# A two-layer diffusion backbone on one core: FFN up-projection as seven block products, FFN in two phases

## Chip, core, metric

One core of one Trainium2 chip. The metric is the device time of one execution in microseconds (us); lower is better. Engines: TensorE (PE; its weight loads are PEld), VectorE (DVE), ScalarE (ACT), GpSimd (POOL), and SyncE (SP), which issues the DMAs.

## What is computed

Two layers act on 512 latent tokens and 256 context tokens of width 1024. Each layer is a mixing sublayer (three groups of heads, one output projection) and a gated FFN with a hidden width of 2816. The last layer's FFN runs on the 512 latent tokens only; layer 0's runs on all 768.

```python
def swiglu(h, w13, w2):
    gate, up = jnp.split(h @ w13, 2, axis=-1)
    return (jax.nn.silu(gate) * up) @ w2
...
for l in range(DEPTH):
    ...
    lat = lat + gt1 * rms_norm(mixed_l, norm_mix_post[l])
    h_l = modulate(rms_norm(lat, norm_ffn_pre[l]), sh2, sc2)
    lat = lat + gt2 * rms_norm(swiglu(h_l, ffn_w13[l], ffn_w2[l]), norm_ffn_post[l])
```

## The kernel before

**Precision.** Every large product is made of three matmuls. An operand is split into a high part (a cast to the matmul's format, done by ACT) and a low part (operand minus high part, done by DVE or POOL); `gemm3` (L383 to L388) then accumulates high·high, high·low and low·high in PSUM.

**Weights.** Weights stream in units of at most 1 MB, in the order of a list (`specs`). `load` (L307 to L329) fetches a unit into `raw` (one buffer), casts `whi` (L327, ACT, up to 2048 columns in one instruction) and subtracts `wlo` (L328, DVE); both have two buffers. `get` (L331) loads one unit ahead.

**Normalized input.** `pre_norm` (L246 to L267) normalizes a tile of 128 tokens, turns it by 8 transposes on PE (L256), applies scale and shift while it leaves PSUM (`hh`, half on ACT, half on DVE) and writes high and low parts into `hT` (ACT L266, POOL L267), which holds all tokens. The output projection is software-pipelined: while PE works on a tile, the tile before is normalized (`out_front`, `out_back`).

**FFN.** The hidden width is 22 blocks of 128. `ffn_up` computes gate and up of a block for all tokens: in layer 0, 48 matmuls of 512 columns (latent tokens) and 48 of 256 (context); in layer 1, 48 of 512. The first two blocks (`ffn_first`) are cut into 256-token pieces, so that they start with the tokens that are already normalized. `ffn_gate` makes silu(gate) (ACT L1130) times up (DVE L1131); `ffn_split` makes the hidden block's high part (ACT L1135) and low part (POOL L1136), which stay in SBUF. After each group of blocks (groups of 2, 4, 4, 4, 4, 4) `ffn_down` multiplies the group by its 512-column halves of `ffn_w2`; a group's result is added to `facc` in SBUF (ACT L1181 for the first, DVE L1183 for the others). In the last group each tile's post-norm, and in layer 0 the pre-norm of layer 1, follow the tile's two halves (`ffn_back`).

**Order.** A tile scheduler places the instructions on the engines' queues from program order; each engine then runs its own queue in order. Side work, the matmuls of the modulation vectors (`pa`, L196 to L210, with 512 KB DMAs `araw`), is put in between at hand-placed points (`ada_some`).

Of the kernel before, what the change touches and what calls it, by code (L numbers as in the profile page):

```python
# [20 lines left out]
D = 1024  # L21
# [62 lines left out]
def tile_backbone(ctx: ExitStack, tc: tile.TileContext, a: dict, out: bass.AP, dbg=None):  # L84
# [5 lines left out]
    wp = ctx.enter_context(tc.tile_pool(name="wp", bufs=2))  # L90
# [37 lines left out]
    hT = [pt(pp, "hThi", [128, 8, T], F32R), pt(pp, "hTlo", [128, 8, T], F32R)]  # L128
    hTf = [h.bitcast(F32) for h in hT]
# [7 lines left out]
    qds = [pt(dp, f"qd{l}", [T, 512]) for l in range(NL)]  # L137

# [107 lines left out]
    def pre_norm(np_, l, k, tb, x):  # L246
# [4 lines left out]
        for j in range(2):  # L251
            ps = px()
            h = pt(np_, "hh", [128, 4, 128])
# [53 lines left out]
    def load(i, hp=None, tag=None):  # L307
        name, shape, srcs, prem, hook = specs[i]
# [3 lines left out]
        rs = f"p ({dims}) -> p {dims}"  # L312
        hp = hp or wp
        lo = pt(hp, "wlo", [128, 2048], F32R)[:, :n].rearrange(rs, **kw)
        hi = pt(hp, "whi", [128, 2048], F32R)[:, :n].rearrange(rs, **kw)
        raw = pt(wp, "raw", [128, 2048], bufs=1)[:, :n].rearrange(rs, **kw)
# [4 lines left out]
        if prem is not None:  # L321
            for kb in range(shape[1]):
                w = cols[prem][:, 66 + kb:67 + kb]
                S.activation(hi[:, kb], raw[:, kb], AF.Copy, scale=w)
                V.scalar_tensor_tensor(lo[:, kb], raw[:, kb], w, hi.bitcast(F32)[:, kb], ALU.mult, ALU.subtract)
        else:
            S.copy(hi, raw)  # L327
            V.tensor_tensor(lo, raw, hi.bitcast(F32), ALU.subtract)  # L328
        state["units"][i] = (hi, lo)  # L329
# [17 lines left out]
    for l in range(NL):  # L347
# [895 lines left out]
```

## Time and profile before

| | |
|---|---|
| median of 3 runs | 1917.22 us (1916.05 to 1921.72) |
| span of the profiled execution | 1910.3 us |
| time of the profiled execution | not given apart from its span; 6.9 us lie between span and median |
| PE busy | 1834.0 us, 96% of the span, 11579 matmuls |
| DVE, ACT, POOL busy | 906.6 us (47%), 670.5 us (35%), 436.5 us (23%) |

The span runs from the first to the last instruction of the execution. Busy time of matmuls is modelled and they overlap in the pipeline, so the time that one matmul costs in a stream is read from the chain of waits (a piece's length by its count), not from its mean duration.

### The profile page before, as it was taken

What the parts mean: (1) busy time and instruction counts of PE and PEld (TensorE: products, weight loads), DVE (VectorE), ACT (ScalarE), POOL (GpSimd) and SP (SyncE); (2) the same over time, 40 slices, a digit from 0 to 9 for tenths busy, and PEclk for the clock granted to TensorE, in tenths of its full rate; (3) what the DMA queues carried; (4) which work ended last, traced back from release to release, by engine and by line L of the source; (5) the groups of instructions that cost most, each with busy time, mean ns of one, the idle gap of its engine ahead of it and who ended that gap; (6) DMA issues with size and microseconds to landing.
All of it is one profiled execution on the core that took longest, in us unless ns stands there. A gap on an engine that the chain in (4) does not pass through costs nothing.

```text
span 1910.3 us, 28279 instructions
## 1 busy us (share of the span) xinstructions
PE 1834.0 (96%) x11579; PEld 1562.8 (82%) x11579; DVE 906.6 (47%) x1594; ACT 670.5 (35%) x1157; POOL 436.5 (23%) x413
## 2 busy tenths in 40 slices
PE   5999999999999999999999989999997999999998
PEld 3789988878998888888888767898896987888886
DVE  4576698747432222322223265739876432332334
ACT  3545453225533212121121265545333542222222
POOL 1103454205321111111010131046322231112112
PEclk9899999999999999999999998999997999999999
DMA  8335344546352222222222363343423343333232
GB/s 281 114 111 161 114 144 139 176 148 218 132 165 87 68 77 78 66 63 70 67 89 62 93 214 102 97 138 112 133 86 108 110 159 110 88 102 97 89 90 87
DMA packets 242941, 221.71 MB, mean 116 GB/s; under 512 B 12024, under 2 KB 218844, under 8 KB 242684
## 3 DMA queue, kind: packets, MB, share of 16 engines
q1 hardware_dynamic: 241744, 218.60, 36.3%
q8 instruction: 91, 1.49, 0.3%
q10 hardware_dynamic: 1068, 1.31, 0.2%
q14 instruction: 38, 0.31, 0.1%
HBM read 197.99 MB, written 21.89 MB: 115 GB/s over the span
## 4 chain that ended last, share of the span: by engine, by line
PE 80%; DVE 9%; DMA 4%; ACT 3%; issue 2%; POOL 1%; SPq 0%; POOLq 0%; DVEq 0%; ACTq 0%
PE mm L388 46%; PE px L388 22%; PE pa L196 2%; PE px L906 2%; DVE wlo L328 1%; DMA araw<-ada_w_dram 1%; DVE W L672 1%; PE px L256 1%; PE px L635 1%; DMA vd<-stg 1%; ACT whi L327 1%; DVE E L666 1%; DMA xa<-x_dram 1%; PE px L844 1%; PE px L840 1%
## 5 line engine op out<-in xcount | busy, mean ns | idle before, releaser
L388 PE MATMUL mm<-hThi,whi 128*128 128x512 f32 (+2 forms) x1384 | 483.9, 350 | 4.0 <-ACT hThi L443 3.5
L388 PE MATMUL mm<-hTlo,whi 128*128 128x512 f32 (+2 forms) x1384 | 481.9, 348 | 3.0 <-DVE hTlo L444 2.3
L388 PE MATMUL mm<-hThi,wlo 128*128 128x512 f32 (+2 forms) x1384 | 481.2, 348 | 0.3 <-DVE wlo L328 0.2
L327 ACT CAST whi<-raw 128x2048 fp32r<-128x2048 f32 (+2 forms) x96 | 177.4, 1848 | 430.6 <-PE mm L388 197.2
L388 PEld LDWEIGHTS mm<-hThi,whi 128*128 128x128 f32 (+1 forms) x1384 | 260.1, 188 | 52.5 <-issue 8.7
L328 DVE TENSOR_TENSOR wlo<-raw,whi 128x2048 fp32r<-128x2048 f32 (+2 forms) x96 | 216.8, 2258 | 171.2 <-ACT whi L327 170.9
L388 PEld LDWEIGHTS mm<-hTlo,whi 128*128 128x128 f32 (+1 forms) x1384 | 260.4, 188 | 42.7 <-DVE hTlo L444 2.6
L1136 POOL TENSOR_TENSOR hidlo<-hf,hidhi 128x768 fp32r<-128x768 f32 (+1 forms) x44 | 126.6, 2878 | 731.8 <-ACT hidhi L1135 731.8
L388 PEld LDWEIGHTS mm<-hThi,wlo 128*128 128x128 f32 (+1 forms) x1384 | 260.5, 188 | 37.6 <-DVE wlo L328 1.4
L1131 DVE TENSOR_TENSOR hf<-mm,hf 128x512 f32<-128x512 f32 (+1 forms) x63 | 37.7, 598 | 397.7 <-PE mm L388 387.5
L388 PE MATMUL mm<-whi,hThi 128*128 128x256 f32 x688 | 200.7, 292 | 5.6 <-ACT stg L747 3.2
L388 PE MATMUL mm<-whi,hTlo 128*128 128x256 f32 x688 | 198.4, 288 | 0.0
L388 PE MATMUL mm<-wlo,hThi 128*128 128x256 f32 x688 | 198.2, 288 | 0.0
L388 PE MATMUL px<-wlo,hidhi 128*128 128x512 f32 x440 | 174.6, 397 | 0.0
L388 PE MATMUL px<-whi,hidhi 128*128 128x512 f32 x440 | 174.5, 398 | 0.0
L388 PE MATMUL px<-whi,hidlo 128*128 128x512 f32 x440 | 174.0, 397 | 0.0
L388 PEld LDWEIGHTS mm<-whi,hThi 128*128 128x128 f32 x688 | 131.8, 192 | 15.8 <-ACT stg L747 5.1
L388 PEld LDWEIGHTS mm<-wlo,hThi 128*128 128x128 f32 x688 | 131.8, 192 | 2.9 <-issue 1.9
L388 PEld LDWEIGHTS mm<-whi,hTlo 128*128 128x128 f32 x688 | 131.7, 191 | 2.7 <-issue 1.9
L1183 DVE TENSOR_TENSOR facc<-facc,px 128x512 f32<-128x512 f32 x100 | 68.2, 685 | 129.1 <-PE px L388 129.1
L1130 ACT ACTIVATE hf<-mm 128x512 f32<-128x512 f32 (+1 forms) x63 | 32.9, 522 | 246.9 <-PE mm L388 246.9
L388 PEld LDWEIGHTS px<-whi,hidhi 128*128 128x128 f32 x440 | 83.2, 189 | 20.5 <-issue 0.8
(270 smaller groups left out, 2852.5 us busy)
## 6 DMA issues: line engine op xcount, KB each, us to landing
araw<-ada_w_dram SPq DMA_DIRECT2D x96, 512.0 KB
raw<-ffn_w_dram SPq DMA_DIRECT2D x92, 512.0 KB
raw<-w_in_dram SPq DMA_DIRECT2D x26, 1024.0 KB
raw<-ffn_w_dram SPq DMA_DIRECT2D x20, 1024.0 KB
Rt<-gd SPq DMA_DIRECT2D x40, 256.0 KB
raw<-w_out_dram SPq DMA_DIRECT2D x8, 1024.0 KB
xsd<-x SPq DMA_DIRECT2D x16, 512.0 KB
x<-xsd SPq DMA_DIRECT2D x14, 512.0 KB
```

The source lines that it names most:

```text
L196: PE.matmul(ps[32 * g:32 * g + 32, 0:256], sil[:, 4 * kq + g, :], raws[kq][:, g, :], start=kq == 0, stop=kq == 1)
L256: PE.transpose(ps[:, 128 * q:128 * q + 128], xn[:, 128 * kb:128 * kb + 128], ident)
L327: S.copy(hi, raw)
L328: V.tensor_tensor(lo, raw, hi.bitcast(F32), ALU.subtract)
L388: PE.matmul(ps, x(k), y(k), start=(k == 0 and p == 0), stop=(k == n - 1 and p == 2))
L635: PE.matmul(pst[:, 256 * g:256 * g + 256], bt[:, 128 * g:128 * g + 128], xw[:, 256 * g:256 * g + 256], start=True, stop=True)
L666: V.scalar_tensor_tensor(E[:, h], Rt[:, 0, h], gcol[:, tb, hh:hh + 1], E[:, h], ALU.subtract, ALU.min)
L906: PE.matmul(ps[h][:, cs], XX[rr, 1, cs], XX[rr, 0, cs], start=True, stop=True)
L1130: S.activation(hf[:, t0:t0 + n], pg[:, :n], AF.Silu)
L1131: V.tensor_tensor(hf[:, t0:t0 + n], pu[:, :n], hf[:, t0:t0 + n], ALU.mult)
L1136: G.tensor_tensor(hh[1], hf, hh[0].bitcast(F32), ALU.subtract)
L1183: V.tensor_tensor(ac, ac, ps, ALU.add)
```

## The change

**Seven products.** For each hidden block the weights are split into four: a11, a12 are the gate's columns for the lower and upper half of the 1024 inputs, a21, a22 those of up. The normalized input is split into b11, b12 (lower inputs, first and second half of the tokens) and b21, b22 (upper inputs). Sums s1 to s4 of the weights and t1 to t4 of the input are formed, and seven products replace eight; each is 4 input blocks by 3 matmuls of half the tokens (384 columns in layer 0, 256 in layer 1), so 84 matmuls per block. The results are put together from PSUM and SBUF by ACT and DVE, multiplied on POOL, and the hidden block is stored to DRAM (`hds`).

**Weights.** Weights are split in halves of 1024 columns, with four buffers in place of two. `load13` fetches a block's four quarters by two DMAs of 512 KB, forms s3 and a21+a22 on POOL, s2 and s4 on DVE, and splits 3584 columns in four pieces (2048 before).

**FFN start.** `hT` gives way to a rotating pool `H`; the normalized FFN input is held whole in F32 (`whole`), and after the last tile it is turned into 7 operands with high and low parts and 4 differences, each in two halves.

**Down phase.** When all 22 blocks are stored, `hid_pair` reads two blocks at a time back from DRAM, once for each 512-column half of the output, splits them (ACT; DVE and POOL), and `down` accumulates all blocks in PSUM, one bank per tile, with no additions in SBUF. The first half is copied to `y0`; post-norms follow the tiles of the second half's last group.

```diff
-    wp = ctx.enter_context(tc.tile_pool(name="wp", bufs=2))
+    wp = ctx.enter_context(tc.tile_pool(name="wp", bufs=4))
...
+    hds = [pt(dp, f"hd{l}", [NF, 128, T if l + 1 < NL else TL]) for l in range(NL)]
...
+    def load13(i, srcs):
+        F = state["F"]
+        raw = wtile(wp if i % 2 else F, "raw", [128, 4, 512])
+        for dsl, src in srcs:
+            DMA.dma_start(raw[:, dsl].rearrange("p s (k n) -> p (s k) n", n=128), src)
+        a21, a22, a11, a12 = (raw[:, q] for q in range(4))
+        sm = pt(F, "S", [128, 3, 512], bufs=1)
+        s2, s3, s4 = (sm[:, q] for q in range(3))
+        G.tensor_tensor(s3, a11, a21, ALU.subtract)
+        G.tensor_tensor(a21, a21, a22, ALU.add)
+        V.tensor_tensor(s2, a21, a11, ALU.subtract)
+        V.tensor_tensor(s4, a12, s2, ALU.subtract)
+        t0 = split(wp, raw[:, 2:4], [128, 2, 512], V)
+        t1 = split(wp, sm[:, 0:2], [128, 2, 512], V)
+        t2 = split(wp, raw[:, 0:2], [128, 2, 512], V)
+        t3 = split(wp, sm[:, 2:3], [128, 1, 512], V)
...
+            rsplit("b11", bhi[:, 0], blo[:, 0], b11, V)
+            rsplit("b21", bhi[:, 1], blo[:, 1], b21, V)
+            vsub(t1, b12, b11)
+            vsub(t2, b22, t1)
+            vsub(t3, b22, b12)
+            vsub(t4, b21, t2)
+            rsplit("b22", bhi[:, 2], blo[:, 2], b22, V)
+            tlo = pt(hp, "H", [128, 4, 4, hn], F32R)
+            for nm, q in (("t2", 1), ("t3", 2), ("t1", 0), ("t4", 3)):
+                rsplit(nm, thi[:, q], tlo[:, q], tm[:, q], V)
...
+                pa = mm()
+                prod(pa, un, "a11", "b11", True)
+                uu = ut("uu")
+                S.copy(uu, pa[:, :hn])
+                pb = px()
+                prod(pb, un, "s2", "t2", True)
+                V.tensor_tensor(uu, uu, pb[:, :hn], ALU.add)
+                pc = px()
+                prod(pc, un, "s3", "t3", True)
+                u3 = ut("u3")
+                V.tensor_tensor(u3, uu, pc[:, :hn], ALU.add)
+                pd = px()
+                prod(pd, un, "s1", "t1", True)
+                V.tensor_tensor(h2, u3, pd[:, :hn], ALU.add)
+                prod(pa, un, "a12", "b21", False)
+                g1 = ut("g1")
+                S.activation(g1, pa[:, :hn], AF.Silu)
+                prod(pc, un, "a22", "t4", False)
+                V.tensor_tensor(h1, uu, pc[:, :hn], ALU.add)
+                G.tensor_tensor(h1, h1, g1, ALU.mult)
+                prod(pd, un, "s4", "b22", False)
+                V.tensor_tensor(uu, uu, pd[:, :hn], ALU.add)
+                g2 = ut("g1")
+                S.activation(g2, uu, AF.Silu)
+                G.tensor_tensor(h2, h2, g2, ALU.mult)
+                DMA.dma_start(hds[l][f], hf)
...
+            def hid_pair(f):
+                hr = pt(Dp, "hr", [128, 2, tot], bufs=2)
+                DMA.dma_start(hr, hview[:, f:f + 2])
+                hh = [pt(Dp, t, [128, 2, tot], F32R, bufs=3) for t in ("hidhi", "hidlo")]
+                for q in range(2):
+                    S.copy(hh[0][:, q], hr[:, q])
+                    (G if q else V).tensor_tensor(hh[1][:, q], hr[:, q], hh[0][:, q].bitcast(F32), ALU.subtract)
+                return hh
...
+            for j in range(2):
+                pss = accs(j)
...
+                        for k0 in range(0, gn, 2):
+                            hh = hid_pair(f + k0)
+                            for pos in range(npos):
+                                down(pss[pos], hh, un, k0, pos, f + k0)
```

Where the FFN of layer 0 begins, TensorE's queue before: `px_5907` and `px_5919` take the last tile's transposes, `mm_6042` and `mm_6043` are gate and up of the first block on the context tokens, `px_6094` its gate on the first 256 latent tokens.

```order
L388 MATMUL mm_6042<-hTlo_84,whi_6035 128x256
L388 MATMUL mm_6042<-hThi_83,wlo_6034 128x256 [waits DVE_49]
L388 MATMUL mm_6042<-hThi_83,whi_6035 128x256
L388 MATMUL mm_6042<-hTlo_84,whi_6035 128x256 [waits Pool_49]
...
L210 MATMUL pa_5996<-cst_75,arow_6005 128x2 [waits Activation_49]
L388 MATMUL mm_6043<-hThi_83,wlo_6034 128x256
L256 MATMUL px_5907<-cst_75,xn_5905 128x128 [waits Activation_49]
L256 MATMUL px_5907<-cst_75,xn_5905 128x128 x3
L256 MATMUL px_5919<-cst_75,xn_5905 128x128 x4
L388 MATMUL px_6094<-hThi_83,whi_6035 128x256
L388 MATMUL px_6094<-hTlo_84,whi_6035 128x256 [waits Pool_49]
```

Now: `px_5948` and `px_5957` take the last tile's transposes, `mm_6158` is a11·b11 and then a12·b21 of the first block, `px_6173`, `px_6187` and `px_6202` are the products with t2, t3 and t1 (`H_6071` their high parts, `H_6092` their low parts).

```order
L203 MATMUL pa_6050<-araw_6046,sil_102 32x256 x3
L266 MATMUL px_5948<-cst_75,xn_5946 128x128 [waits Activation_49]
L266 MATMUL px_5957<-cst_75,xn_5946 128x128 x4
L1211 MATMUL mm_6158<-bhi_6068,whi_6117 128x384 [waits Activation_49]
L1211 MATMUL mm_6158<-blo_6069,whi_6117 128x384 [waits DVE_49]
L1211 MATMUL mm_6158<-bhi_6068,wlo_6118 128x384 [waits DVE_49]
...
L1211 MATMUL px_6173<-H_6071,whi_6121 128x384 [waits Activation_49]
L1211 MATMUL px_6187<-H_6071,whi_6121 128x384
L1211 MATMUL px_6202<-H_6071,whi_6125 128x384 [waits Activation_49]
L1211 MATMUL mm_6158<-bhi_6068,whi_6117 128x384 [waits Activation_49]
L1211 MATMUL mm_6286<-bhi_6068,whi_6141 128x384 [waits Activation_49]
L1211 MATMUL px_6173<-H_6092,whi_6121 128x384 [waits DVE_49]
```

Before, matmuls of the FFN stood ahead of the last transposes; now every product stands behind them, and the first that uses a low part of a t stands behind the two halves of the first gate product.

At the same place DVE's queue now: L274 writes the last tile's normalized input (`H_4983` is `whole`), L1194 forms t1 to t4 in `tm_6070`, L1190 subtracts low parts (`blo_6069` of b, `H_6092` of t), L329 and L369, L370 are the first block's weights.

```order
L274 TENSOR_SCALAR H_4983<-px_5948,modc0_134 128x128 [waits Activation_49]
L1194 TENSOR_TENSOR tm_6070<-H_4983 128x768 [waits DMAHW0_49,DVE_49,Pool_49]
L1190 TENSOR_TENSOR blo_6069<-H_4983,bhi_6068 128x768 [waits DMAHW5_49,DMAHW2_49,Activation_49]
...
L1190 TENSOR_TENSOR blo_6069<-H_4983,bhi_6068 128x768 [waits Activation_49]
L329 TENSOR_TENSOR wlo_6118<-raw_6109,whi_6117 128x1024 [waits DMAHW1_49,Activation_49]
L369 TENSOR_TENSOR S_6112<-raw_6109 128x512 [waits DMAHW0_49,Pool_49]
L329 TENSOR_TENSOR wlo_6122<-S_6112,whi_6121 128x1024 [waits Activation_49]
L329 TENSOR_TENSOR wlo_6126<-raw_6109,whi_6125 128x1024 [waits Activation_49]
L329 TENSOR_TENSOR wlo_6130<-S_6112,whi_6129 128x512 [waits Activation_49]
L1190 TENSOR_TENSOR H_6092<-tm_6070,H_6071 128x768 [waits DVE_49]
L1190 TENSOR_TENSOR H_6092<-tm_6070,H_6071 128x768 x6
```

None of the L1194 and L1190 rows stood there before; `px_6173`'s wait on DVE above is for the first row that writes `H_6092`.

Where the up phase of layer 0 ends, SP's queue now: `hf` is a finished hidden block on its way to DRAM (`hd0_100`), `raw` a unit of `ffn_w2`, `hr` a pair of blocks on its way back.

```order
L342 DMA raw_8821<-ffn_w2_dram 128x2x512 [waits DMAHW3_49,DMAHW6_49,DMAHW2_49,DVE_49]
L1246 DMA hd0_100<-hf_8717 128x768 [waits DMAHW7_49,Pool_49]
L342 DMA raw_8946<-ffn_w2_dram 128x4x512 [waits DMAHW6_49,DMAHW0_49,DVE_49]
L1246 DMA hd0_100<-hf_8831 128x768 [waits DMAHW1_49,Pool_49]
L1258 DMA hr_8956<-hd0_100 128x2x768 [waits PE_49]
L342 DMA raw_9000<-ffn_w2_dram 128x4x512 [waits DMAHW0_49,DVE_49]
```

Before, SP had no hidden block to move; now the first pair's load stands behind the last block's store.

## Rows read from the trace of the kernel before

**Rows 1.** The page, part 1: busy time of each engine.
```profile
PE 1834.0 (96%) x11579; PEld 1562.8 (82%) x11579; DVE 906.6 (47%) x1594; ACT 670.5 (35%) x1157; POOL 436.5 (23%) x413
```

**Rows 2.** Part 4: the chain that ended last, by engine and line.
```profile
PE 80%; DVE 9%; DMA 4%; ACT 3%; issue 2%; POOL 1%; SPq 0%; POOLq 0%; DVEq 0%; ACTq 0%
PE mm L388 46%; PE px L388 22%; PE pa L196 2%; PE px L906 2%; DVE wlo L328 1%; DMA araw<-ada_w_dram 1%; DVE W L672 1%; PE px L256 1%; PE px L635 1%; DMA vd<-stg 1%; ACT whi L327 1%; DVE E L666 1%; DMA xa<-x_dram 1%; PE px L844 1%; PE px L840 1%
```

**Rows 3.** Stretches: both FFNs, an idle spell, the passage between layers.
```profile
core 0: us, PE busy (x) PEld busy (x) DVE busy (x) ACT busy (x) POOL busy (x), PEclk, DMA share, GB/s
532.50:1080.00 547.50, 544.96 (x2991) 459.19 (x2991) 137.68 (x147) 115.02 (x132) 76.30 (x29) 1.00 0.26 78
1528.00:1893.60 365.60, 363.60 (x1657) 296.72 (x1656) 120.25 (x106) 99.11 (x104) 68.80 (x30) 1.00 0.34 102
539.80:547.00 7.20, 4.66 (x32) 3.22 (x32) 2.30 (x5) 2.17 (x4) 1.93 (x3) 0.76 1.05 321
1094.50:1158.20 63.70, 53.17 (x332) 40.81 (x332) 33.26 (x63) 40.35 (x75) 22.33 (x30) 0.87 0.66 222
```

**Rows 4.** The chain by time (start, length, what): unbroken FFN streams.
```profile
560.54 14.95 PE px L388 x126
...
632.82 17.04 PE mm L388 x96
...
1576.97 44.99 PE mm L388 x192
```

**Rows 5.** The same chain where the FFN of layer 0 begins.
```profile
532.71 2.60 PE mm L388 x21
...
536.42 6.87 DMA araw<-ada_w_dram
...
544.35 1.90 PE px L256 x8
...
546.25 2.10 PE px L388 x15
```

**Rows 6.** The same chain where the FFN of layer 1 begins.
```profile
1526.23 5.05 DMA raw<-ffn_w_dram
...
1535.67 2.88 PE pa L388 x22
...
1538.55 0.60 PE px L256 x4
```

**Rows 7.** Instructions by line and shape (count, busy us, mean ns).
```profile
L328 DVE TENSOR_TENSOR wlo<-raw,whi 128x1024 fp32r<-128x1024 f32 x4 | 5.2, 1311 | 6.7 <-ACT whi L327 6.5
...
L1183 DVE TENSOR_TENSOR facc<-facc,px 128x512 f32<-128x512 f32 x100 | 68.2, 685 | 129.1 <-PE px L388 129.1
...
L444 DVE TENSOR_TENSOR hTlo<-xT,hThi 128x768 fp32r<-128x768 f32 x4 | 3.8, 956 | 1.0 <-ACT hThi L443 0.8
...
L1131 DVE TENSOR_TENSOR hf<-mm,hf 128x256 f32<-128x256 f32 x22 | 9.3, 424 | 52.5 <-PE mm L388 42.3 <-issue 10.2
...
L327 ACT CAST whi<-raw 128x1024 fp32r<-128x1024 f32 x4 | 4.2, 1048 | 11.7 <-PE mm L388 9.0 <-DMA raw<-ffn_w_dram 2.7
...
L681 POOL TENSOR_TENSOR y<-xs,dsk 128x512 f32<-128x512 f32 x10 | 10.5, 1056 | 106.8 <-DMA Rt<-gd 96.5 <-DVE z L700 10.3
...
L267 POOL TENSOR_TENSOR hTlo<-hh,hThi 128x512 fp32r<-128x512 f32 x32 | 44.4, 1395 | 45.6 <-ACT hThi L266 41.4 <-PE pa L196 1.6 <-DVE y L280 1.4
```

**Rows 8.** Timeline, FFN of layer 1: GpSimd beside VectorE, and alone.
```profile
1616.59 2.88 POOL L1136 TENSOR_TENSOR hidlo<-hf,hidhi 128x512 fp32r<-128x512 f32 x1 [6.43 <-ACT hidhi L1135]
...
1616.02 2.29 DVE L328 TENSOR_TENSOR wlo<-raw,whi 128x2048 fp32r<-128x2048 f32 x1 [4.47 <-ACT whi L327]
...
1530.51 1.29 POOL L267 TENSOR_TENSOR hTlo<-hh,hThi 128x512 fp32r<-128x512 f32 x1 [1.34 <-ACT hThi L266]
```

**Rows 9.** The chain again: exposed weight splits, first and last of nine.
```profile
246.51 1.61 DVE wlo L328
...
1360.34 2.19 DVE wlo L328
```

More of the change, by code (lines that the diff above doesn't have):

```diff
@@ L252, in pre_norm @@
             ps = px()
-            h = pt(np_, "hh", [128, 4, 128])
+            if whole is None:
+                h = pt(np_, "hh", [128, 4, 128])
+            else:
+                h = whole[:, 4 * j:4 * j + 4, 128 * pos:128 * pos + 128]
             for q in range(4):
@@ L320, in load @@
             DMA.dma_start(raw[dsl], src)
[L321 to L329, printed above, removed]
+        nb = shape[1]
@@ new lines, in load @@
+        step = max(1, nb // 2)
+        parts = []
+        for k0 in range(0, nb, step):
+            psh = [128, step] + list(shape[2:])
+            if prem is None:
+                parts.append(split(hp, raw[:, k0:k0 + step], psh, V))
+                continue
+            hi, lo = wtile(hp, "whi", psh), wtile(hp, "wlo", psh)
+            for k in range(step):
+                w = cols[prem][:, 66 + k0 + k:67 + k0 + k]
+                S.activation(hi[:, k], raw[:, k0 + k], AF.Copy, scale=w)
+                V.scalar_tensor_tensor(lo[:, k], raw[:, k0 + k], w, hi.bitcast(F32)[:, k], ALU.mult, ALU.subtract)
+            parts.append((hi, lo))
@@ new lines, in tile_backbone, with halves, rsplit @@
+            b11, b12 = whole[:, 0:4, 0:hn], whole[:, 0:4, hn:tot]
+            b21, b22 = whole[:, 4:8, 0:hn], whole[:, 4:8, hn:tot]
+            t1, t2, t3, t4 = (tm[:, q] for q in range(4))
+            rhs = {}
+            def halves(fn, *aps):
+                for k in (0, 2):
+                    fn(*(ap[:, k:k + 2] for ap in aps))
+            def rsplit(nm, hi, lo, src, eng):
+                halves(S.copy, hi, src)
+                halves(lambda o, x, y: eng.tensor_tensor(o, x, y, ALU.subtract), lo, src, hi.bitcast(F32))
+                rhs[nm] = hi, lo
@@ L1139, in ffn_up, with prod, ut @@
+            def prod(ps, un, wn, rn, first):
+                w, r = un[wn], rhs[rn]
+                for k in range(4):
+                    for p, (x, y) in enumerate(((0, 0), (0, 1), (1, 0))):
+                        PE.matmul(ps[:, :hn], w[x][:, k], r[y][:, k], start=first and k == 0 and p == 0,
+                                  stop=k == 3 and p == 2, skip_group_check=True)
+            def ut(tag):
+                return pt(F, tag, [128, hn], bufs=2)
             def ffn_up(f):
```

266 lines of the change are left out of this document (129 added, 137 removed).

## The prediction

> **What bounds the kernel now.** I read the shares first: TensorE is busy 96% of the span and no other engine half of it [rows 1], and the chain of waits runs through TensorE for 80%, 68% of the span in the matmuls of line 388 alone [rows 2]. Then the stretches: in the FFN of layer 0 TensorE idles 2.5 us of 547.5, in that of layer 1 2.0 us of 365.6, both at granted clock 1.00, while VectorE is busy 137.68 and 120.25 us [rows 3]. So the two FFNs, 913 us, are a plain stream of matmuls, and each matmul removed there gives back its pitch. The chain gives the pitches: 14.95 us for 126 matmuls of 256 columns is 118.7 ns, 44.99 us for 192 of 512 is 234.3 ns [rows 4]. Between them I put 384 columns at 176.5 ns. The reader should see the reverse as well: whatever now makes TensorE wait inside these stretches is paid in full.
>
> All sums are made against the profiled execution; 6.9 us lie between its span, 1910.3 us, and the median, 1917.2 us, and I add differences to the median. About 0.3% (5.8 us) is what a measurement can tell from no change.
>
> **Fewer columns.** A block's up-projection in layer 0 took 17.04 us [rows 4]; now 84 matmuls of 384 columns take 84 x 0.1765 = 14.83 us. Over 22 blocks: -2.21 x 22 = -48.7 us. In layer 1 a block took 44.99 / 4 = 11.25 us; 84 x 0.1187 = 9.97 us. -1.28 x 22 = -28.1 us. Together -76.8 us, if TensorE never waits. This gain is firm to some 3 us, the uncertainty of the interpolated pitch.
>
> By the Trainium skill ("TensorE: Matmul & The Clock Gate", Back-to-back issue gap) an isolated warm matmul takes N/2.4 + 2.5 ns, 109, 162.5 and 216 ns for the three widths, and the gain would be 22 x (15.6 - 13.65) + 22 x (10.35 - 9.17) = -69 us; the trace's pitches are 8% above it, so it is not used.
>
> **Start of layer 0's FFN.** Before, 48 FFN matmuls of 256 columns ran ahead of the last transposes, and the stream flowed at 546.25 us [rows 5]: as if it had begun at 546.25 - 48 x 0.1187 = 540.5. Now nothing of the FFN can start before the last tile is normalized, since each operand spans half of all tokens, and VectorE then has a queue ahead of the first low part of a t: 14 half operands of 768 columns at 0.956 us, three weight pieces at 1.311, three of 512 columns at 0.685 [rows 7], and four evacuations at the 0.4 of a 256-column read from PSUM: 13.4 + 3.9 + 2.1 + 1.6 = 21.0 us, and one more half. The transposes end at the same 546.25, because what they follow (a modulation chunk's DMA of 6.87 us [rows 5]) stays. So the low part is there at 568.2; TensorE has done 29 matmuls (5.1 us) by then, effective start 563.1, +22.6 us. With 2 us for GpSimd's weight sums in the way (below): +25. The least is +10, if the scheduler's queue lets the b parts be made under the output projection and ScalarE and VectorE overlap well; the most +32.
>
> **Start of layer 1's FFN.** Before, TensorE went from one sublayer into the other almost without a gap [rows 3, 6]. Now the same queue with 512-column halves: 14 x 0.685 + 3.9 + 2.1 + 1.6 + 0.7 = 17.9 us after the last transposes at 1539.2 [rows 6], less 29 x 0.1187 = 3.4 us of matmuls done: 1553.7 against an effective 1530.6 (1528.0, 2.0 idle, 0.6 of transposes): +23, with GpSimd +26. Ends +10 and +33.
>
> **From up to down.** The first pair of blocks is read behind the last block's store, and its buffers lie where the up phase's were. After the last product: an addition (0.5), silu (0.5), the product on GpSimd (0.8 from 1.056 for 512 columns), issue, a transfer of 0.5 to 0.75 MB (1 MB took 5.05 us [rows 6]; 4.5), a cast (0.8) and the queue steps between: +8.5 in layer 0, +7 in layer 1. Inside the phase a pair needs 8.4 us of TensorE in layer 0 (36 matmuls of 234 ns) and 5.6 in layer 1, and reads 1.25 and 1 MB, at most 190 GB/s, where 321 GB/s was seen [rows 3]; I cost the reload at nothing. Its cover is two buffers of pairs; without it each pair would show some 5 us. The 100 additions into facc, 68.2 us of VectorE [rows 7], lay beside TensorE and give nothing.
>
> **Layer 1's steady blocks.** VectorE's work per block, from [rows 7]: weight low parts 3 x 1.311 + 0.685, sums 2 x 0.685, five additions from PSUM at 0.424: 8.1 us of 9.97. GpSimd: two sums at 1.056, two products of 256 columns at 0.53: 3.2 us. Each fits alone. But GpSimd's 512-column subtraction took 2.88 us when it began beside a 2.29 us weight low part, and 1.29 alone [rows 8]: 1.72 us of waiting, just what was left of VectorE's instruction, then 1.16 of work. If only VectorE's instructions with two SBUF operands exclude GpSimd, 6.0 + 3.2 = 9.2 us fit in 9.97, with little to spare, and the sums feed the low parts in a chain. I take 10.3 us per block: +0.33 x 22 = +7.5. The ends are 0 and +29 (11.3 us). Layer 0's blocks last 14.83 us, against 8.8 + 3.7 of the same work; no stall.
>
> **Clock.** After a spell of idling the granted clock was 0.76 over 7.2 us [rows 3]. Four new idle spells (two starts, two phase borders) at 1.3 us each: +5; 0 to +10.
>
> **Passage between layers.** Half of the last group's matmuls now lie before it, 72 x 0.234 = 16.8 us. But of its 63.7 us ScalarE was busy 40.35 [rows 3], and the normalizing of six tiles stays; I take -10, ends -17 and +10.
>
> **Mixing sublayers.** Nine whole weight casts or subtractions of 1.6 to 2.4 us lie on the chain, the first and the last in [rows 9]; in halves of 1024 columns (1.048 us to cast, 1.311 to subtract [rows 7]) about half of some 18 us goes, and some modulation chunks move from layer 0's FFN into layer 1's mixing, where they are not covered: -5, ends -15 and +10.
>
> **Sum.** -76.8 + 25 + 26 + 15.5 + 7.5 + 5 - 10 - 5 = -12.8 us: 1904 us. Most of what the seven products save goes into two starts at which TensorE waits for VectorE.
>
> **Rivals.** (a) GpSimd and VectorE bind layer 1. If every GpSimd instruction keeps VectorE out, a block takes 8.1 + 3.2 = 11.3 us, 22 us more than my sum: 1926, slower. It turns to a loss above 10.85 us per block (12.8 / 22 over my 10.3). For it: [rows 8]; against: additions from PSUM need not exclude GpSimd. By the Trainium skill ("SBUF — State Buffer", SBUF: two separate sides) a GpSimd instruction and a VectorE one with two SBUF inputs take an exclusive lock for the whole instruction, and the loser blocks; by that rule the 9.2 us hold and the trace's 2.88 us agree. (b) The starts are mostly covered, 10 us each as above: 1904 - 31 = 1873. For it: four of six tiles are normalized long before the last; against: VectorE's queue order. (c) The round trip through DRAM shows in layer 1, where a pair leaves 5.6 us for a 4.5 us transfer, a cast and a subtraction: 1.7 us on each of 22 pairs, +37: 1941. For it: two buffers only; against: the DMA share of 0.34 there [rows 3]. That the change does not do what it says is excluded: the queue shows 84 matmuls a block.
>
> **How the numbers follow.** Forecast 0.45 (own range 1890 to 1920), (a) 0.22, (b) 0.23, (c) 0.10. Range 1862 to 1938: it takes in (a), (b) and the ends of the passage, and leaves out most of (c). Faster by over 0.3% (below 1911): (b) and two thirds of the forecast, 0.54. Within: 0.14, most of it the forecast's. Slower: (a), (c) and a little of the forecast, 0.32.
>
> **What would show it.** In the chain, layer 0 blocks of 14.8 us and layer 1 blocks near 10.3; about 20 us of TensorE idle at each FFN start, released by VectorE's subtractions of line 1190; 7 to 9 us at each phase border, released by a DMA. If layer 1's blocks take over 10.85 us with VectorE or GpSimd as releaser, (a) holds; if the starts cost under 15 us, (b); if line 1270's matmuls wait for the reloaded pairs, (c).

## The result, and the profile after

The changed kernel takes 1897.58 us (median of 4 runs, 1892.41 to 1900.21) against 1916.63 us before (4 runs, 1913.05 to 1921.72): a ratio of 0.990, 95% interval 0.987 to 0.9925. That is 19 us or 1.0% faster. The prediction said 1904 us, range 1862 to 1938.

The profiled execution of the changed kernel has a span of 1897.1 us and took 1899.0 us, so 1.9 us lie outside its span, not the 6.9 us that the prediction read between span and median. If as much lies outside the span of the kernel before, its 1910.3 us belong to an execution of some 1912 us, shorter than any of the four above. The two traces differ by 13.2 us, not 19. The ledger below is made between the traces.

Part 1 of the page, busy time by engine, answers to [rows 1]:

```profile
PE 1768.9 (93%) x11915; PEld 1581.0 (83%) x11915; DVE 1172.1 (62%) x2022; ACT 804.7 (42%) x1462; POOL 587.1 (31%) x569
```

TensorE is busy 65 us less, 93% of the span where it was 96%, VectorE 265 us more, GpSimd 151 us more. Its idle time in the span grew from 76.3 to 128.2 us, so 52 of the 65 us saved are waits now.

The two up phases without their starts, by stretch (length, then busy time of PE, PEld, DVE, ACT, POOL with instruction counts, granted clock, DMA share, GB/s), answer to the FFN rows of [rows 3]:

```profile
core 0: us, PE busy (x) PEld busy (x) DVE busy (x) ACT busy (x) POOL busy (x), PEclk, DMA share, GB/s
587.00:892.00 305.00, 305.00 (x1757) 305.00 (x1756) 178.85 (x230) 106.28 (x146) 95.23 (x83) 1.00 0.32 96
1572.30:1752.00 179.70, 179.70 (x1514) 179.70 (x1513) 147.28 (x199) 83.83 (x127) 94.96 (x71) 1.00 0.43 126
```

TensorE never waits inside either phase, at granted clock 1.00. VectorE is busy 147.28 of 179.70 us in layer 1, 82%, without holding TensorE up. The chain of waits shows the pace; these are the pieces of 12 matmuls in layer 1 that begin every third block (start, length, what):

```profile
1572.34 1.44 PE px L1211 x12
...
1602.29 1.45 PE px L1211 x12
...
1632.24 1.45 PE px L1211 x12
```

29.95 us from one to the next is 9.98 us per block, where the prediction computed 9.97 without stalls and took 10.3 with them. In layer 0 a block's first matmul follows that of the block before by 14.60 us (14.83 forecast), which is 173.8 ns for each of 84 matmuls of 384 columns. Before it was 17.04 and 11.25 us [rows 4].

What is lost is lost at the edges. The start of layer 0's up phase, from SP, ScalarE, GpSimd, VectorE and TensorE in the timeline (start, length, engine and line, instruction, in brackets the idle time before it and what ended it):

```profile
546.93 23.05 SPq L363 DMA_DIRECT2D raw<-ffn_w_dram  x4
...
556.14 1.04 ACT L328 CAST whi<-raw 128x1024 fp32r<-128x1024 f32 x1 [2.62 <-DMA raw<-ffn_w_dram]
...
556.33 5.08 POOL L367 TENSOR_TENSOR S<-raw 128x512 f32<-128x512 f32 x1 [12.54 <-DMA raw<-ffn_w_dram]
...
562.79 0.69 DVE L369 TENSOR_TENSOR S<-raw 128x512 f32<-128x512 f32 x1 [2.52 <-POOL raw L368]
...
569.48 5.30 DVE L1190 TENSOR_TENSOR H<-tm,H 128x768 fp32r<-128x768 f32 x6
...
557.23 0.69 PE L1211 MATMUL mm<-bhi,whi 128*128 128x384 f32 x1 [8.37 <-ACT whi L328]
564.62 0.62 PE L1211 MATMUL px<-H,whi 128*128 128x384 f32 x2 [2.46 <-ACT whi L328]
```

TensorE's first product stands right behind the last transposes, which end at 548.3 us, and waits 8.37 us for ScalarE's cast of the first weights; that cast waited for a transfer which SP could issue only at 546.93 us. GpSimd's first weight sum, which can start no sooner, takes 5.08 us beside VectorE's queue, VectorE then idles 2.5 us for it, and its low parts of t begin at 569.48 us. In layer 1 the first product is held twice, once by the cast and once by the weights' low part on VectorE:

```profile
1523.65 0.58 PE L1211 MATMUL mm<-bhi,whi 128*128 128x256 f32 x1 [4.88 <-ACT whi L328]
...
1529.15 0.58 PE L1211 MATMUL mm<-bhi,wlo 128*128 128x256 f32 x1 [4.70 <-DVE wlo L329]
```

The border between up and down phase in layer 0, SP, ScalarE and TensorE:

```profile
894.88 0.32 SPq L1246 DMA_DIRECT2D hd<-hf  x1
895.25 0.43 SPq L1258 DMA_DIRECT2D hr<-hd  x1
...
899.85 1.56 ACT L1261 CAST hidhi<-hr 128x768 fp32r<-128x768 f32 x2 [3.10 <-DMA hr<-hd]
...
900.73 0.79 PE L1270 MATMUL px<-whi,hidhi 128*128 128x512 f32 x1 [8.15 <-ACT hidhi L1261]
```

The last block's store goes out at 894.88 us, the first pair's load right behind it; the cast waits for that load and TensorE 8.15 us for the cast. (Below, a border's gap is counted from the last product's start plus its pitch: 8.3 us here, 7.6 in layer 1.)

### The profile page after: what moved, and what is told of

It is laid out like the page before. It is cut to its first block, busy times and chain, and to the rows that moved or that the text cites. A ratio compares the mean times of both kernels' runs of the same rounds, so it can differ in the third digit from the quotient of the medians.

```text
span 1897.1 us, 30528 instructions
## 1 busy us (share of the span) xinstructions
PE 1768.9 (93%) x11915; PEld 1581.0 (83%) x11915; DVE 1172.1 (62%) x2022; ACT 804.7 (42%) x1462; POOL 587.1 (31%) x569
## 3 DMA queue, kind: packets, MB, share of 16 engines
q10 hardware_dynamic: 1068, 1.31, 0.2%
## 5 line engine op out<-in xcount | busy, mean ns | idle before, releaser
L329 DVE TENSOR_TENSOR wlo<-raw,whi 128x1024 fp32r<-128x1024 f32 (+2 forms) x192 | 274.7, 1435 | 163.5 <-ACT whi L328 163.2
L1211 PE MATMUL px<-H,whi 128*128 128x384 f32 (+1 forms) x1408 | 310.9, 312 | 5.7 <-ACT whi L328 5.7
L328 ACT CAST whi<-raw 128x1024 fp32r<-128x1024 f32 (+2 forms) x192 | 194.4, 1018 | 241.1 <-PE px L1211 107.5
L433 PE MATMUL mm<-whi,H 128*128 128x256 f32 x1376 | 269.0, 290 | 7.1 <-ACT stg L793 6.4
L1211 PEld LDWEIGHTS px<-H,whi 128*128 128x128 f32 x1408 | 237.3, 191 | 7.4 <-ACT whi L328 7.4
L433 PEld LDWEIGHTS mm<-whi,H 128*128 128x128 f32 x1376 | 219.4, 192 | 21.8 <-ACT stg L793 9.1
L1211 PE MATMUL px<-H,wlo 128*128 128x384 f32 (+1 forms) x704 | 213.9, 311 | 0.0
L433 PE MATMUL mm<-wlo,H 128*128 128x256 f32 x688 | 198.4, 288 | 0.0
L433 PE MATMUL mm<-H,whi 128*128 128x256 f32 (+2 forms) x720 | 179.6, 338 | 5.5 <-DVE H L490 2.6
L433 PEld LDWEIGHTS mm<-wlo,H 128*128 128x128 f32 x688 | 132.4, 192 | 2.4 <-issue 1.3
L1211 PE MATMUL mm<-bhi,whi 128*128 128x384 f32 (+1 forms) x352 | 111.2, 316 | 14.2 <-ACT whi L328 14.2
L329 DVE TENSOR_TENSOR wlo<-S,whi 128x1024 fp32r<-128x1024 f32 x88 | 89.2, 1013 | 47.0 <-ACT whi L328 46.8
```

The source lines that it names most:

```text
L328: S.copy(hi, src)
L329: lo_engine.tensor_tensor(lo, src, hi.bitcast(F32), ALU.subtract)
L433: PE.matmul(ps, x(k), y(k), start=(k == 0 and p == 0), stop=(k == n - 1 and p == 2))
L1211: PE.matmul(ps[:, :hn], w[x][:, k], r[y][:, k], start=first and k == 0 and p == 0, stop=k == 3 and p == 2, skip_group_check=True)
```

## Experiments

Times are medians, ratios are against runs of the kernel before on the same chip. Stage times come from each kernel's trace. Differences from the changed kernel compare medians of runs on different chips; the kernel before had medians of 1916.6 to 1917.7 us on them. "Effective start" is the up phase's end less 22 blocks at its steady pace; the up phase's end is the start of its last matmul plus one pitch.

**e1. First block's weights early.** The first block of each layer took the raw buffer that lies in the FFN's pool; now it takes the one outside.

```diff
-        raw = wtile(wp if i % 2 else F, "raw", [128, 4, 512])
+        raw = wtile(F if i % 2 else wp, "raw", [128, 4, 512])
```

> The first block's weights are loaded into the buffer outside the FFN's pool, so they can be fetched while the output projection still runs; nothing else changes. Theory A (late weights): in the changed kernel the first product waited for ScalarE's cast of weights whose transfer began only at 546.9 us, and GpSimd's sums then stood in the middle of VectorE's queue; the first product should start about 3 us after the last transposes in place of 8.9, and the effective start of the up phase come 5 to 7 us earlier in layer 0 and 3 to 5 us in layer 1: about 1887 us, 8 to 11 us below the changed kernel. Theory B (the prediction's: VectorE's queue of 21 us sets it): the first low part of a t comes at the same distance from the transposes, total within 2 us of the changed kernel.

Measured: 1889.94 us, ratio 0.986 (0.984 to 0.988), 7.6 us below the changed kernel. TensorE, GpSimd and VectorE at layer 0's start:

```profile
548.49 0.69 PE L1211 MATMUL mm<-bhi,whi 128*128 128x384 f32 x1 [0.22 <-ACT bhi L1186]
...
544.05 1.27 POOL L367 TENSOR_TENSOR S<-raw 128x512 f32<-128x512 f32 x1
545.40 1.27 POOL L368 TENSOR_TENSOR raw<-raw 128x512 f32<-128x512 f32 x1
...
565.41 0.69 PE L1211 MATMUL mm<-bhi,wlo 128*128 128x384 f32 x1 [4.34 <-DVE wlo L329]
...
566.26 8.23 DVE L1190 TENSOR_TENSOR H<-tm,H 128x768 fp32r<-128x768 f32 x7
```

The first product starts 0.9 us after the transposes, and GpSimd's sums are done in 1.27 us each before VectorE's queue begins. The effective start, counted from the last transposes, falls from 22.9 to 14.9 us in layer 0 and from 16.3 to 14.2 in layer 1. Theory A holds for 8 us in layer 0 and 2 in layer 1 (5 to 7 and 3 to 5 expected). Of the 14.9 us that remain in layer 0, 0.9 lie before the first product, 7.2 are waits behind it and 6.9 are matmuls that ran at the lower granted clock (more on this below). The longest of the waits, 4.34 us, is for a low part, and the low parts of t begin at 566.26 us only.

**e2. One difference in place of four.** It leaves out part of the computation: t2, t3 and t4 take the value of t1.

```diff
-            vsub(t2, b22, t1)
-            vsub(t3, b22, b12)
-            vsub(t4, b21, t2)
...
-                rsplit(nm, thi[:, q], tlo[:, q], tm[:, q], V)
+                rsplit(nm, thi[:, q], tlo[:, q], tm[:, 0], V)
```

> Leaves out part of the computation: only t1 is formed, and t2, t3, t4 take its value, so 6 of the 8 half subtractions on VectorE at each FFN start are gone. Theory B (VectorE's queue): the starts shorten by 6 x 0.95 = 5.7 us in layer 0 and 6 x 0.68 = 4.1 us in layer 1, total about 10 us below the changed kernel, 1888 us. Theory A (late weights): layer 0 gains under 2 us, since VectorE then waits for the weights' sums longer; layer 1 up to 3; total 1893 to 1897 us.

Measured: 1889.69 us, ratio 0.986 (0.984 to 0.988), 7.9 us below. From the last transposes the effective start falls by 6.1 us in layer 0 (5.7 expected by theory B) and by 3.0 in layer 1 (4.1). So the queue on VectorE is on the path as well: the weights' sums and the operands' sums stand in one line, and taking either out shortens it.

**e3. Low parts on GpSimd.**

```diff
-                rsplit(nm, thi[:, q], tlo[:, q], tm[:, q], V)
+                rsplit(nm, thi[:, q], tlo[:, q], tm[:, q], G if nm in ("t1", "t4") else V)
```

> The low parts of t1 and t4 (four half subtractions in each layer) go from VectorE to GpSimd. If the two engines work side by side, VectorE's queue is shorter by 3.8 us in layer 0 and 2.7 in layer 1, and the total 3 to 6 us below the changed kernel. If they exclude each other while both read SBUF operands, GpSimd's instructions show durations far over their 1.3 to 2 us, the low parts come later, and the total is the same or up to 8 us above.

Measured: 1908.57 us, ratio 0.995 (0.993 to 0.997), 11 us above the changed kernel. The group of the moved instructions, and in the timeline the stretch in which they run, GpSimd first:

```profile
L1190 POOL TENSOR_TENSOR H<-tm,H 128x768 fp32r<-128x768 f32 x4 | 13.3, 3349 | 5.2 <-DVE tm L1194 5.2
```

```profile
569.29 7.86 POOL L1190 TENSOR_TENSOR H<-tm,H 128x768 fp32r<-128x768 f32 x1 [5.21 <-DVE tm L1194]
...
577.11 5.47 POOL L1190 TENSOR_TENSOR H<-tm,H 128x768 fp32r<-128x768 f32 x3
...
570.80 3.56 DVE L1190 TENSOR_TENSOR H<-tm,H 128x768 fp32r<-128x768 f32 x4
574.27 1.22 DVE L329 TENSOR_TENSOR wlo<-raw,whi 128x1024 fp32r<-128x1024 f32 x1
582.65 0.55 DVE L1227 TENSOR_TENSOR uu<-uu,px 128x384 f32<-128x384 f32 x1 [7.16 <-PE px L1211]
```

The mean of 3.35 us hides two cases. GpSimd's first subtraction took 7.86 us: it began inside VectorE's chain, which ran on without a break until 575.49 us, four subtractions in 3.56 us. Its other three took 1.8 us each, with VectorE idle and waiting for TensorE. So GpSimd waited for VectorE's chain, and the rest of the step then hung on GpSimd alone. The total is 3 us worse than the worse of the two expected cases. The effective start is 1.9 us later in layer 0 and 3.8 in layer 1; some of the rest lies in the mixing sublayers (2.4 us by layer 0's last output projection), which the edit does not touch but whose order on the queues differs from kernel to kernel, as below.

**e4. Eight products in the same two phases.** No weight sums, no t; gate and up of each token half as two products each.

```diff
+                for h, c in ((h1, "1"), (h2, "2")):
+                    pa = mm()
+                    prod(pa, un, "a11", "b1" + c, True)
+                    prod(pa, un, "a12", "b2" + c, False)
+                    g1 = ut("g1")
+                    S.activation(g1, pa[:, :hn], AF.Silu)
+                    pc = px()
+                    prod(pc, un, "a21", "b1" + c, True)
+                    prod(pc, un, "a22", "b2" + c, False)
+                    V.tensor_tensor(h, g1, pc[:, :hn], ALU.mult)
```

> The same two phases, halved weight pieces and seven-product storage, but eight plain products per block (96 matmuls of 384 or 256 columns), no sums of weights, no t. Against the changed kernel the up phase gets 22 x 12 matmuls longer in each layer: 22 x 12 x 0.174 = 45.9 and 22 x 12 x 0.119 = 31.4 us, and the starts shorter by what VectorE no longer does (about 9 us in layer 0 and 7 in layer 1): 1897.6 + 77 - 16 = 1959 us, 2.2% above the kernel before. If the starts are dearer than VectorE's queue alone, down to 1945 us; if the starts do not depend on the t at all, 1975 us.

Measured: 1955.58 us, ratio 1.020 (1.017 to 1.024). Its steady stretches, in the columns used above:

```profile
590.00:900.00 310.00, 310.00 (x1790) 310.00 (x1790) 66.37 (x75) 55.18 (x74) 0.00 (x0) 1.00 0.28 84
1580.00:1800.00 220.00, 220.00 (x1870) 220.00 (x1869) 63.19 (x78) 53.36 (x78) 0.00 (x0) 1.00 0.38 112
```

A block takes 16.64 and 11.31 us, against 14.60 and 9.98 with seven products, and the effective start lies 8.7 and 8.1 us after the transposes, against 22.9 and 16.3. So the seven products by themselves give 22 x (2.04 + 1.33) = 74 us and cost 22 us at the starts, 52 us net. The medians differ by 58; 4.3 us of the rest are this kernel's longer borders (gaps of 10.4 and 9.4 us before TensorE's first matmul of the down phases, 8.15 and 7.39 in the changed kernel). The rest of the change (two phases, halved weight pieces) with eight plain products is 2% slower than the kernel before, and with the seven products the whole is 1% faster.

**e5. Chunks held back.** Twelve modulation chunks, in program order placed between the blocks of layer 0's up phase. A chunk is 16 matmuls in the trace; the scheduler put five of the twelve into the up phase and six fewer before the end of layer 0's last output projection (384 of the chunks' matmuls in place of 480).

```diff
-                ada_some(adp, 2)
+                ada_some(adp, 2 if last else min(2, len(todo) - 12))
...
-        ada_some(adp, len(todo))
...
                 ffn_up(f)
+                if f % 2 == 0:
+                    ada_some(adp, 1 if f < 20 else len(todo))
```

> Twelve modulation chunks of layer 0 (those that nothing before the FFN's end needs) are held back and placed between the blocks of layer 0's up phase, as the kernel before had some of them inside its FFN. Theory C (the mixing sublayer lost because chunks came forward into it): layer 0's output projection ends 4 to 6 us earlier against 537.0, the last transposes no longer wait for a chunk's transfer (2 to 3 us), the up phase gets 8 to 11 matmul groups of 0.6 to 1 us longer: total 2 to 6 us below the changed kernel, 1892 to 1896 us. Rival D (the loss is the scheduler's order of other work): output projection at 536 to 538 as before, total within 2 us or above, since the up phase only gets longer.

Measured: 1898.9 us, ratio 0.990 (0.987 to 0.992): no change that can be told from the changed kernel's. In total that is rival D's side. But the pieces moved as theory C says, and by more: layer 0's last output projection ends at 523.9 us in place of 537.0, and from the second block on a block of the up phase takes 15.12 us in place of 14.60, 10.4 us over 20 blocks. Of the 13 us that the mixing sublayer gains, the up phase takes back most, since it has no idle TensorE time. It pays more than the chunks' own time. Two of a chunk's matmuls, alone between a block's, make that block 0.73 us longer (15.33 us), where 16 in a row take 1.07 us (both from this run's trace):

```profile
524.70 1.07 PE L203 MATMUL pa<-araw,sil 128*32 128x256 f32 x16
...
610.71 0.62 PE L203 MATMUL pa<-araw,sil 128*32 128x256 f32 x2
```

In the changed kernel the chunks' price shows where the output projection should begin; TensorE's queue stands behind a chunk whose weights are still on their way:

```profile
452.24 1.08 PE L203 MATMUL pa<-araw,sil 128*32 128x256 f32 x8 [4.39 <-DMA araw<-ada_w_dram]
```

**e6. Pairs read back early.**

```diff
+                if f == 9 or last and f == 11:
+                    early[f - 9] = hr_load(f - 9, None)
...
-                hr = pt(Dp, "hr", [128, 2, tot], bufs=2)
-                DMA.dma_start(hr, hview[:, f:f + 2])
+                hr = early.pop(f, None)
+                if hr is None:
+                    hr = hr_load(f, Dp)
```

> The buffers of the reloaded hidden blocks lie outside the up phase's pool, and the first pair (in layer 1 the first two) is fetched in the middle of the up phase, not behind the last store. Theory E (the border waits for the round trip through DRAM): the gap from last product to first down matmul falls from 8.3 and 7.6 us to 2 to 4 in both layers, and layer 1's down phase loses 2 us less behind its late second pair: total 9 to 12 us below the changed kernel, 1886 to 1889 us. Rival F (the border waits for memory of the up phase to come free and for the casts): 5 us of gap remain, total 3 to 5 us below.

Measured: 1889.92 us, ratio 0.985 (0.983 to 0.987), 7.7 us below. The gap falls from 8.3 to 5.1 us in layer 0 and from 7.6 to 6.2 in layer 1. SP, ScalarE and TensorE at layer 0's border:

```profile
888.29 0.38 SPq L342 DMA_DIRECT2D raw<-ffn_w_dram  x1
...
893.36 1.99 ACT L328 CAST whi<-raw 128x1024 fp32r<-128x1024 f32 x2 [0.92 <-DMA raw<-ffn_w_dram]
895.26 1.56 ACT L1273 CAST hidhi<-hr 128x768 fp32r<-128x768 f32 x2
...
896.14 0.79 PE L1282 MATMUL px<-whi,hidhi 128*128 128x512 f32 x1 [4.90 <-ACT hidhi L1273]
```

The pair is there; now the casts of the first `ffn_w2` unit, fetched only from 888.29 us on, stand ahead of it on ScalarE's queue. So the border is nearer to rival F, though what it waits for is the weights. The two gaps are 4.6 us shorter, but the down phases behind them are 2.3 us longer (188.0 and 127.2 us in place of 186.8 and 126.1), so the borders explain 2.3 of the 8 us. Between the traces, which differ by 8.2 us, 1.3 of the others lie before the end of layer 0's up phase and 4.6 in the passage and layer 1's mixing sublayer, where the order on the queues differs again.

**e7. Whole weight units.** One cast and one subtraction of up to 2048 columns per unit outside the up-projection, as in the kernel before.

```diff
-    wp = ctx.enter_context(tc.tile_pool(name="wp", bufs=4))
+    wp = ctx.enter_context(tc.tile_pool(name="wp", bufs=2))
...
-        step = max(1, nb // 2)
+        step = nb
```

> Weights outside the up-projection are split in whole units again (one cast and one subtraction of 2048 columns, two buffers), as in the kernel before; the up-projection's pieces share buffers in pairs. If halving the pieces gave the 8 us that the changed kernel is ahead of the kernel before at 240 us of layer 0's mixing, this kernel is within 2 us of the kernel before there; if the lead came from elsewhere it stays 6 to 9 us. The up phase may lose by its coarser buffers; only the mixing sublayers are compared.

Measured: one run, 1905.23 us. The comparison is of the mixing sublayer of layer 0. For TensorE's instructions other than the chunks', where they exist unchanged in both kernels, the table has how much later (+) or earlier (-) they start than in the kernel before (median over those within 5 us of the time at the left, in us):

```
time before   changed   whole units   chunks held
        150     -4.0          +0.2          -3.8
        240     -8.7          +0.5          -8.4
        260     -2.3          +0.5          -2.8
        320     -3.3          -0.6          -3.8
        400     -1.4          +0.3          -4.7
        450     -0.7          +0.2          -4.2
        510     +5.6          +0.6          -7.9
        536     +5.6          +0.6          -7.6
```

With whole units the sublayer is the old one to within 0.6 us throughout. So both the lead that halved pieces win by 240 us and its loss come with the halved pieces. The lead goes in two places. Between 240 and 260 us 6 us of it go, with the chunks held back as well: TensorE waits there for a copy by ScalarE, and ScalarE had waited for a DMA that stores what it copied before. These are TensorE and ScalarE in the changed kernel, then TensorE with the chunks held back; the kernel before has no wait there:

```profile
251.40 0.41 PE L433 MATMUL mm<-whi,H 128*128 128x256 f32 x1 [4.89 <-ACT stg L793]
...
250.97 0.37 ACT L793 COPY stg<-mm 128x256 f32<-128x256 f32 x1 [6.46 <-DMA qd<-stg]
...
250.88 0.39 PE L433 MATMUL mm<-whi,H 128*128 128x256 f32 x1 [4.14 <-ACT stg L793]
```

Behind 320 us the two kernels part, and after 450 us, at the chunk shown under e5, the changed kernel falls behind the kernel before.

**e8 to e11. Combinations.** e8 has the edits of e1, e5 and e6, e9 those of e1 and e6; e10 and e11 add one edit each to e9.

> First block's weights early, chunks in layer 0's up phase, and first pair read back early, together. If the three gains add: -7.6 (measured) with -4 (chunks) and -10 (reload) against 1897.6: 1876 us, 0.979 of the kernel before. If chunks give nothing and the border waits for memory: 1886 us.

Measured: 1888.51 us, ratio 0.985 (0.983 to 0.986). The three gains do not add: chunks in the up phase cost there most of what they free (15.11 us per block).

> First block's weights early (as in e1) and first pair read back early (as in e6), no change to the modulation chunks. If the two gains are separate they add: -7.6 and -7.7 against 1897.6, 1882 us, 0.982 of the kernel before. If the order of the mixing sublayers that each run happened to get was part of either gain, 1886 to 1889 us.

Measured: 1884.1 us (1881.94 to 1892.99), ratio 0.984 (0.981 to 0.986): the fastest kernel of this study by its median, 13.5 us below the changed kernel, 33.6 below the kernel before, and between the two cases expected. Its profiled execution is its longest run, so its stages are not compared. It is not told apart from e1 and e6 by the intervals.

> As e9, and seven modulation chunks of layer 0 are held back until the FFN's start, where TensorE waits for VectorE, not placed between blocks. Theory C: layer 0's output projection ends some 6 to 8 us earlier (half of what twelve gave), the up phase keeps its 14.6 us per block, total 4 to 8 us below e9. Rival: the chunks' transfers (1 MB each) and their matmuls stand ahead of the last transposes and the first products, the start gets later by as much as the mixing gains: total within 2 us of e9.

```diff
-                ada_some(adp, 2)
+                ada_some(adp, 2 if last else min(2, len(todo) - 7))
...
-        ada_some(adp, len(todo) - 12)
+        ada_some(adp, len(todo) - (12 if last else 7))
...
                 ffn_up(f)
+                ada_some(adp, 2)
```

Measured: 1887.66 us, ratio 0.986 (0.984 to 0.988), 3.6 us above e9: nearer the rival's side. The last transposes come 13.6 us after the output projection's end, 11.3 in the changed kernel, and the chunks fill the place where the first products should be prepared.

> As e9, with the two weight sums of each block moved from GpSimd to VectorE. VectorE's work per layer-1 block rises from 8.2 to 9.6 us, under the 9.98 us of TensorE. If the exclusion of the two engines is what their sums cost, GpSimd's spans fall, nothing waits and the total is equal or up to 3 us below e9. If VectorE's queue becomes the bound (chains of sums, casts and low parts leave gaps in it), layer 1's blocks take 10.2 to 10.8 us, the starts 1 to 2 us longer, and the total is 6 to 20 us above e9.

```diff
-        G.tensor_tensor(s3, a11, a21, ALU.subtract)
-        G.tensor_tensor(a21, a21, a22, ALU.add)
+        V.tensor_tensor(s3, a11, a21, ALU.subtract)
+        V.tensor_tensor(a21, a21, a22, ALU.add)
```

Measured: 1891.03 us, ratio 0.987 (0.985 to 0.989), 7 us above e9 by the medians with intervals that overlap. A stretch of layer 1's up phase, in the same columns:

```profile
1570.00:1730.00 160.00, 160.00 (x1345) 160.00 (x1344) 142.70 (x209) 75.91 (x112) 38.43 (x32) 1.00 0.45 134
```

VectorE is busy 89% and TensorE still never waits; a block takes 10.01 us. Layer 1's blocks do not turn on where the sums are made. What the 7 us are is not shown.

## Why the prediction was right

The forecast of -12.8 us stands beside -13.2 us between the traces; the measured terms below add up to -13.8. That it came out so closely is luck: the steady blocks and layer 0's columns were 12.5 us better than their terms, the mixing sublayers 12.7 us worse.

| term, us | forecast | measured | where it is read |
|---|---|---|---|
| fewer columns, layer 0 | -48.7 | -53.7 | 22 x (17.04 - 14.60) |
| fewer columns, layer 1 | -28.1 | -27.9 | 22 x (11.25 - 9.98) |
| start, layer 0 | +25 | +28.6 | effective start 571.2, transposes 2.1 later than before |
| start, layer 1 | +26 | +22.7 | effective start 1535.0, from the output projection's end |
| two borders | +15.5 | +15.9 | gaps of 8.3 and 7.6 |
| layer 1's steady blocks | +7.5 | 0 | 9.98 us per block |
| clock after idling | +5 | +3.6 | the borders' part alone: down phases of 186.8 and 126.1 us, over 792 and 528 x 0.2343 |
| passage between layers | -10 | -10.7 | lead over the kernel before grows from 13.5 us (layer 0's rows above, with its 2.1 us of mixing) to 24.2 in layer 1's first matmuls |
| mixing sublayers | -5 | +7.7 | 2.1 at layer 0's last transposes, 5.6 in layer 1 |

**Fewer columns.** The gain was sized rightly. A matmul of 384 columns takes 173.8 ns, not the 176.5 put between its neighbours, which is worth 5 us.

**Starts.** The sizes held, the reason only in part. The prediction put all but 2 us of layer 0's start down to VectorE's queue; the trace and e1 show that 8 of the 28.6 us are the first block's weights, which the buffer's place in the FFN's pool keeps from being fetched early. The excerpt of VectorE's queue ahead of the prediction has the weight sums standing in it with a wait on GpSimd. e2 shows that VectorE's subtractions are on the path, at about the prediction's price in layer 0 (6.1 us for 5.7) and below it in layer 1 (3.0 for 4.1).

The clock was sized too small. The prediction counted the matmuls of both starts at their full pitch and gave each idle spell 1.3 us. After the waits of each start and of each border the granted clock was 0.50, the lower of its two levels (1.2 GHz); stretches of the changed kernel, in the columns used above:

```profile
552.00:562.00 10.00, 4.42 (x12) 3.57 (x12) 8.27 (x10) 7.31 (x11) 5.59 (x2) 0.50 0.18 54
900.70:903.50 2.80, 2.77 (x7) 2.19 (x8) 0.96 (x1) 0.71 (x1) 1.86 (x1) 0.50 1.05 410
1523.70:1538.40 14.70, 9.46 (x39) 8.58 (x40) 14.70 (x21) 8.99 (x15) 1.83 (x2) 0.50 0.00 1
1762.30:1767.00 4.70, 4.69 (x11) 3.74 (x12) 1.68 (x2) 1.61 (x3) 4.04 (x3) 0.50 1.01 401
```

Of the 22.9 us from layer 0's last transposes to its effective start, 8.9 lie before the first product, 7.1 are later waits, and 6.9 are matmuls that took longer than 173.8 ns; of layer 1's 16.3 us the parts are 4.9, 6.0 and 5.5. How much of the 6.9 and 5.5 us a full clock would give back no run shows, since a faster matmul may only wait longer for VectorE.

**Steady blocks.** This term fell away whole, and with it rival (a) (whose loss begins at 10.3 + 12.8 / 22 = 10.88 us per block, not 10.85). VectorE's sum per block was right (8.1 forecast, 147.28 / 18 = 8.2 measured), GpSimd's spans rose to 94.96 / 18 = 5.3 us from the 3.2 that the prediction added up, and TensorE waited for neither. e11 loads VectorE to 89% with the same result. The groups of the changed kernel (count, busy time, mean ns) show who pays:

```profile
L367 POOL TENSOR_TENSOR S<-raw 128x512 f32<-128x512 f32 x44 | 70.3, 1598 | 43.8 <-DVE wlo L329 24.2 <-DMA raw<-ffn_w_dram 12.5 <-ACT bhi L1186 7.1
...
L329 DVE TENSOR_TENSOR wlo<-raw,whi 128x1024 fp32r<-128x1024 f32 x180 | 261.4, 1456 | 149.9 <-ACT whi L328 149.8
```

Sums of 512 columns took 1.6 us on the mean (1.06 for the like of the kernel before [rows 7], 1.27 for e1's first, beside an idle VectorE), and VectorE's 1024-column low parts 1.46 for 1.31. The Trainium skill ("SBUF — State Buffer", SBUF: two separate sides) has such instructions exclude each other for a whole instruction; the stretched spans on both engines agree, and so does e3's first subtraction, which ended only behind VectorE's chain. The work of two SBUF operands, 6.0 + 3.2 = 9.2 us, fitted into 9.98 as that rule has it.

**Mixing sublayers.** This is the step that failed: -5 us forecast, +7.7 measured. "About half of some 18 us goes" held only until 240 us of layer 0, where the lead was 8.7 us, near the half; then it was lost. The prediction named the modulation chunks as the price, and layer 1's mixing as the place where they are not covered. That was half right. These are the chunks' matmuls from the start to the end of layer 0's last output projection, in the kernel before, in the changed one and in e5, then from layer 1's first projections to the end of its output projection, before and changed:

```profile
core 0: us, PE busy (x) PEld busy (x), PEclk, DMA share, GB/s
0.00:531.50 531.50, 44.57 (x480) 13.98 (x480) 0.98 0.49 158
0.00:537.10 537.10, 47.18 (x480) 14.50 (x480) 0.97 0.49 155
0.00:524.00 524.00, 36.91 (x384) 11.39 (x384) 0.98 0.46 147
1158.50:1527.40 368.90, 6.33 (x64) 1.95 (x64) 0.95 0.34 107
1133.90:1508.90 375.00, 15.61 (x160) 5.14 (x160) 0.96 0.38 123
```

Layer 1 did get six chunks more, 9.3 us of TensorE's busy time, and lost 5.6 us net. Layer 0 has as many as before. It lost 14.3 us between 240 us and the output projection's end, part of it to the wait for ScalarE's copy at 251.40 us, part to the wait for a chunk's transfer at 452.24. e5, with six chunks fewer in the sublayer, ends it 13 us earlier; that is the price of the chunks there, not proof that they caused the loss. Why the order with halved pieces leads to these waits stays open.

**Borders, passage, clock.** Borders and passage came within 1 us of their terms; the passage is what its neighbours in the ledger leave, not a wait that was measured. Of the clock, the 3.6 us are the two borders' part; that of the starts stands in their rows. e6 refines the border: behind the reloaded pair stand the weights' casts, so an early reload alone takes 3 of 8 us off the gap.

**Rivals.** Rival (b), starts covered, did not happen by itself; e1 shows that over a quarter of layer 0's start could be covered by moving one buffer. Rival (c) shows nowhere inside the down phases, which exceed their matmuls by 1.2 and 2.4 us.

What stays open: how much of a total difference of 3 to 8 us between two variants is the order that their mixing sublayers happen to get. Between the kernels whose edits lie in the FFN alone, their length differs by up to 6 us in layer 0 and by some 8 in layer 1.

## What to carry to other kernels

A saving of matmul columns is paid in full where TensorE is the bound, and so is every wait that the new form puts at a stage's edges: price the edges with the same care, counting each engine's queue from the last event before them. Where a start looks long, ask of each input separately when its transfer could first be issued; a buffer's place in a pool can decide that. Work that fills another engine's waits, like the modulation chunks here, costs at least its full time as soon as it is put into a stretch without waits, and more when it is put there in small pieces (0.73 us for two of e5's chunk matmuls, 1.07 for 16 in a row).

## What the hardware showed that was not expected

An instruction of GpSimd that began beside a running chain of VectorE subtractions waited until the chain broke. In layer 0's start of the changed kernel one 512-column sum took 9.15 us beside such a chain, and another 5.08 (shown above); the sum behind the first, with the chain over, took 1.28. VectorE was not always the one that went on: in e1 two of its 768-column subtractions, 0.95 us each elsewhere in the chain, took 1.93 and 2.03 us beside GpSimd's sums. GpSimd in the changed kernel, then VectorE in e1:

```profile
569.64 9.15 POOL L367 TENSOR_TENSOR S<-raw 128x512 f32<-128x512 f32 x1 [6.89 <-DVE wlo L329]
578.87 1.28 POOL L368 TENSOR_TENSOR raw<-raw 128x512 f32<-128x512 f32 x1
...
566.26 1.93 DVE L1190 TENSOR_TENSOR H<-tm,H 128x768 fp32r<-128x768 f32 x1
...
568.11 2.03 DVE L1190 TENSOR_TENSOR H<-tm,H 128x768 fp32r<-128x768 f32 x1
```
